# Gated DeltaNet and squared-ReLU MLP layer in float32 on one core: where the substitution rows, the query norms and the output roots of a head pair stand in the program

## Chip, cores and metric

One core of a Trainium2 chip runs the whole kernel. The metric is the device time of one execution in microseconds (us). Most executions agree within 0.3%.

## What is computed

The input x is one sequence of 2048 tokens with 1024 features, in float32. DEPTH is 1, so there is one layer: RMS norm, gated DeltaNet mixer, residual, RMS norm, squared-ReLU MLP (1024 to 4096 to 1024), residual, and a final RMS norm. The reference of the mixer, cut to what matters:

```python
def gated_deltanet(h, w_in, conv_w, a_log, dt_bias, norm_w, w_out):
    proj = h @ w_in
    qkv = silu(causal_depthwise_conv(proj[..., :3 * DN_WIDTH], conv_w))      # 4 taps
    z, b, a = rest_of(proj)
    q, k, v = split(qkv)                                                     # 8 heads of 128
    q, k = l2_normalize(q), l2_normalize(k)
    beta, g = sigmoid(b), -exp(a_log) * softplus(a + dt_bias)
    o = chunk_gated_delta_rule(q, k, v, beta, g)
    o = o * rsqrt(mean(o * o) + eps) * norm_w * silu(z)
    return o @ w_out

def chunk_gated_delta_rule(q, k, v, beta, g):          # per head and chunk
    lower = strict_lower(k_beta @ k.T * decay)
    u, w = solve(I + lower, [v * beta, k_beta * exp(gc)])
    attn = (q @ k.T) * decay
    # then, chunk after chunk:
    v_new = u - w @ state
    o_c = q_dec @ state + attn @ v_new
    state = state * g_last + k_dec.T @ v_new
```

## The kernel before, in words

The kernel works on chunks of 128 tokens. The sequence goes in two blocks of 1024 tokens (`TB`). For each block `mixer` runs, then `mlp_block`. A mixer has two halves of 512 tokens (`s` = 0, 1), and each half has four pairs of heads (`HP` = 2), so there are 16 pairs in all, of 8 chunk matrices each (`NC` = 2 heads times 4 chunks).

**One pair.** Six projections (`conv_part`, counted by n = 1 to 6: k, q and v of both heads) are each 24 matmuls of 128x512 on PE (`dense`, L117 to L119: each float32 product is three matmuls of split parts). ACT then copies the PSUM bank twice (L302, L303), DVE runs three taps of the convolution (L306), ACT a tanh (L309) and DVE the last product (L310). After n = 3 and n = 4 `key_matrices` makes the strictly lower matrices `mt`. Also after n = 4, `invert_diagonal` (L312) starts to invert the 32x32 diagonal blocks: ACT spreads `mt` into `xc` by four copies (L320), DVE transposes it (L323), and 31 substitution rows follow, each one product and one reduction on DVE (L330, L332). After n = 5 and n = 6 `query_norms` (L436) squares the queries of one head on ACT (`sq`, L440) and sums them on PE by four thin matmuls with a column of ones (L442). DVE adds epsilon (L444).

**The pair before it.** When all six projections of a pair are recorded, `wind_up` (L582) handles the previous pair: `prepare2` calls `invert`, which completes the 128x128 inverse from the small blocks by 32-wide and 64-wide matmuls (L358, L365, L368, L377, L382) with copies `z` on ACT between (L360, L379). It also transposes k and v (L457) and makes the attention matrix (L465). `chain` is the recurrence over four chunks (L483 to L500), and after it come the root mean squares of the output (L505 to L513), one head after the other, each with its own `rsqrt` (L126). `gate` projects the gate z of both heads, 24 matmuls of 128x512 each; these wide matmuls stand between the small ones of `invert` and `chain`. `finish` transposes the output and multiplies it by the gate.

**What sets the order.** A scheduler takes the instructions in the order in which the code records them, as a priority, and lays out one fixed queue for each engine, so that an instruction recorded late can stand earlier on an engine that would otherwise idle by the scheduler's own estimates. On the chip each engine works through its queue in order, and whatever stands behind a waiting instruction waits too. PSUM banks: two for projections (`pj`), two for most small products (`kq`), two for the recurrence (`ch`), two for outputs (`po`).

Of the kernel before, what the change touches and what calls it, by code (L numbers as in the profile page):

```python
# [7 lines left out]
F32 = mybir.dt.float32  # L8
# [25 lines left out]
def tile_kernel(ctx: ExitStack, tc: tile.TileContext, x, w_in, w_out, w_up, w_down, n_mlp, n_fin, consts, out):  # L34
# [274 lines left out]
        act.activation(th, dst, AF.Tanh, scale=0.5)  # L309
        dve.scalar_tensor_tensor(dst, th, 1.0, dst, op0=ADD, op1=MULT)  # L310

    def invert_diagonal(ap, mt):  # L312

        R = 32 // NC
        xc = wp.tile([P, 32, R, NC], F32, name="xc", tag="xt", bufs=4)
        for b in range(4):
            r = slice(32 * b, 32 * b + 32)
            act.copy(xc[r], mt[r, :, 32 * b:32 * b + 32].rearrange("p t i -> p i t").unsqueeze(2)  # L320
                     .to_broadcast([32, 32, R, NC]))
        pr = wp.tile([P, 32, 32], F32, name="pr", tag="xt", bufs=4)
        dve.transpose(pr.rearrange("p i j -> p (i j)"), xc.rearrange("p i r t -> p (i r t)"))  # L323
        pool.memset(pr.rearrange("p i j -> p (i j)")[:, 0:1024:33], 1.0)
        tt = ap.tile([P, NC, 32], F32, name="tt", tag="tt")
        pool.tensor_copy(tt.rearrange("p c j -> p (c j)"), e0)
        tmp = ap.tile([P, NC, 32], F32, name="tmp", tag="tmp", bufs=1)
        for i in range(1, 32):
            n = i // R + 1
            dve.tensor_tensor(tmp[:, 0:n, 0:i + 1], tt[:, 0:n, 0:i + 1],  # L330
                              pr[:, i, 0:i + 1].unsqueeze(1).to_broadcast([P, n, i + 1]), op=MULT)
            dve.tensor_reduce(tt[:, 0:n, i], tmp[:, 0:n, 0:i + 1], axis=mybir.AxisListType.X, op=ADD)  # L332
        return tt

    def invert(ap, mt, tt, uf, t64):

# [49 lines left out]
    def sl(t):  # L386
        return slice(t * P, (t + 1) * P)
# [55 lines left out]
        c = NC + j * HT  # L443
        dve.tensor_scalar_add(u["n2"][:, c:c + HT], ps[:, 0:HT], 4.0 * EPS)  # L444

    def prepare2(ap, sb, h, q2, k2, v2, gt, u, ub, t64):
        c0 = h * HT
        dt_, rk = u["dt"], u["rk"]
        invert(ap, u["mt"], u["tt"], ub, t64)
        qe = row(ap, eg_d, "qe", sb, c0)  # L450
        (dve if c0 == NH * HT - NC and sb % 2 else pool).tensor_tensor(flat(qe), flat(qe), q2, op=MULT)
        kt, vt = head(ap, "kt"), head(ap, "vt")
        for dst, src, sc in ((vt, v2, lambda c: rk[:, c:c + 1]), (kt, k2, lambda c: gt["egl"][:, c0 + c:c0 + c + 1])):
            for hf in range(2):
                ps = big("kq")
                for t in range(HT):
                    pe.transpose(ps[:, sl(t)], src[:, sl(hf * HT + t)], ident)  # L457
                for t in range(HT):
                    c = hf * HT + t
                    act.activation(dst[:, c, :], ps[:, sl(t)], AF.Copy, scale=sc(c))  # L460
        for hf in range(2):
            ps = big("kq")
            for t in range(HT):
                s = sl(hf * HT + t)
                pe.matmul(ps[:, sl(t)], k2[:, s], q2[:, s], start=True, stop=True)  # L465
            cs = slice(hf * HT, (hf + 1) * HT)
            dve.tensor_tensor(flat(dt_[:, cs, :]), ps, flat(dt_[:, cs, :]), op=MULT)
        u.update(ub=ub, qe=qe, kt=kt, vt=vt, at=dt_, k2=k2, gt=gt, c0=c0)

    def chain(ap, h0, u):  # L470

        def col(name, c):
            return u["gt"][name][:, u["c0"] + c:u["c0"] + c + 1]
# [2 lines left out]
        for t in range(HT):  # L476
            ts_ = slice(t * P, (t + 1) * P)
            cs = [j * HT + t for j in range(HP)]
            st = [S[h0 + j] for j in range(HP)]
            ys, vrs = [], []  # L480
            for j, c in enumerate(cs):
                ps = big("ch")
                pe.matmul(ps[:, 0:P], u["k2"][:, c * P:(c + 1) * P], st[j], start=True, stop=True)  # L483
                y = ap.tile([P, P], F32, name="y", tag="y")
                dve.scalar_tensor_tensor(y, ps[:, 0:P], col("neg", c), u["vt"][:, c, :], op0=MULT, op1=ADD)
                ys.append(y)
            for j, c in enumerate(cs):
                pe.matmul(po[j][:, ts_], u["qe"][:, c, :], st[j], start=True, stop=False)
            for j, c in enumerate(cs):
                ps = big("ch")  # L490
                pe.matmul(ps[:, 0:P], u["ub"][:, c, :], ys[j], start=True, stop=True)
                vr = ap.tile([P, P], F32, name="vr", tag="vr")
                act.activation(vr, ps[:, 0:P], AF.Copy, scale=u["cc"][:, c:c + 1])
                vrs.append(vr)
            for j, c in enumerate(cs):
                ps = big("ch")
                pe.matmul(ps[:, 0:P], u["kt"][:, c, :], vrs[j], start=True, stop=True)
                dve.scalar_tensor_tensor(st[j], st[j], col("egt", c), ps[:, 0:P], op0=MULT, op1=ADD)
            for j, c in enumerate(cs):
                pe.matmul(po[j][:, ts_], u["at"][:, c, :], vrs[j], start=False, stop=True)  # L500
        os_ = []
        for j in range(HP):
            ms = sm.tile([P, HT], F32, name="ms", tag="ms")
            o = ap.tile([P, HT, P], F32, name="o", tag="o")
            for t in range(HT):  # L505
                act.activation(o[:, t, :], po[j][:, t * P:(t + 1) * P], AF.Square, accum_out=ms[:, t:t + 1])
            nq = sm.tile([P, HT], F32, name="nq", tag="nq")
            dve.tensor_scalar_mul(nq, u["n2"][:, NC + j * HT:NC + (j + 1) * HT], EPS * P)
            dve.scalar_tensor_tensor(nq, ms, 1.0 / P, nq, op0=MULT, op1=ADD)
            rq = sm.tile([P, HT], F32, name="rq", tag="rq")  # L510
            rsqrt(rq, nq)
            for t in range(HT):
                act.activation(o[:, t, :], po[j][:, t * P:(t + 1) * P], AF.Copy, scale=rq[:, t:t + 1])  # L513
            os_.append(o)
        return os_

    def gate(ap, hT, h, sb):
# [51 lines left out]
    def mixer(blk, hT):  # L569
        with tc.tile_pool(name="ap", bufs=2) as ap:  # L570
# [8 lines left out]
                    finish(*r)  # L579
                ready.clear()  # L580

            def wind_up(sb, h, hT, qkv, gt, u):  # L582
                prepare2(ap, sb, h, *qkv, gt, u, ub, t64)
                os_ = chain(ap, h, u)
                return [(sb, h + j, os_[j], gate(ap, hT, h + j, sb)) for j in range(HP)]

            gt = None
            for s in range(2):
                sb = 2 * blk + s
                for h in range(0, NH, HP):  # L590
# [3 lines left out]
                    for part in (1, 0, 2):  # L594
                        d = ap.tile([P, HP * HB], F32, name=f"c{part}", tag=f"c{part}")
                        qkv.append(d)
                        for j in range(HP):
# [12 lines left out]
                            if n == 4:  # L610
                                key_matrices(u, qkv[0], 1)
                                key_norms(u)
                                u["tt"] = invert_diagonal(ap, u["mt"])
                                finish_ready()
                            if n == 5:
                                query_norms(ap, u, qkv[1], 0)
                            if n == 6:
                                query_norms(ap, u, qkv[1], 1)
                            if blk == 0 and s == 1 and n in (2, 5):
                                split_out(h // HP * 2 + n // 5)  # L620
                            if s == 0 and n == 1:
# [241 lines left out]
```

## Time and profile before

| | us |
|---|---|
| three runs, median | 3015.39 |
| three runs, lowest and highest | 3009.5 and 3017.04 |
| the profiled execution, its own time | 3014.35 |
| its span in the profile | 3012.3 |
| PE busy | 2845.6 (94%) |
| DVE busy | 1582.8 (53%) |
| ACT busy | 1023.5 (34%) |
| POOL busy | 731.6 (24%) |

The span is the time from the first to the last instruction; 2.05 us of the execution lie around it. Times in the trace count from the start of the span. PE is the matmul engine; a busy PE can still run at half its clock, so its busy share has to be read together with the granted clock (PEclk). The two mixers stand at about 40 to 760 us and 1590 to 2205 us, the MLP stages after each of them.

### The profile page before, as it was taken

The page shows a single profiled execution, that of the slowest core. Times are in us where ns is not written, and L with a number is a line of the kernel's source. Part 1 is how long each engine was busy: PE and PEld are TensorE (multiplying, and loading weights), DVE is VectorE, ACT ScalarE, POOL GpSimd, SP SyncE. Part 2 cuts the span into 40 slices and gives each one's busy share as a digit, 9 for nine tenths or more (in the row PEclk, how much of TensorE's full clock was granted, in tenths as well). Part 3 has the DMA queues.
Part 4 walks back from the last instruction along what each step waited for, and adds up shares of the span by engine and source line. Part 5 has one row for each costly group of instructions (what it writes and reads, how often), then busy time and mean ns, then how long its engine had stood idle before and what let it go on. Part 6 is the DMA issues. An engine that isn't in the chain of part 4 may idle for free.

```text
span 3012.3 us, 40577 instructions
## 1 busy us (share of the span) xinstructions
PE 2845.6 (94%) x15352; PEld 2390.5 (79%) x15352; DVE 1582.8 (53%) x4054; ACT 1023.5 (34%) x2338; POOL 731.6 (24%) x646
## 2 busy tenths in 40 slices
PE   7888989889999999999999999999999999999998
PEld 5677777778978888888887778888888888888887
DVE  7787676665333333333387767666543333333334
ACT  4454544444221111111146555554532111111112
POOL 6443221110043323323311111010003233233221
PEclk9888988889999999999999999888899999999999
DMA  6544443446621111111144334333563111111111
GB/s 254 171 152 153 144 161 140 161 172 210 215 75 49 36 56 55 43 43 56 57 167 177 127 119 148 132 122 129 173 214 126 43 57 46 39 56 52 46 43 63
DMA packets 81844, 337.66 MB, mean 112 GB/s; under 512 B 8816, under 2 KB 17264, under 8 KB 60144
## 3 DMA queue, kind: packets, MB, share of 16 engines
q1 hardware_dynamic: 60528, 292.98, 28.6%
q10 hardware_dynamic: 21120, 42.08, 4.1%
q8 instruction: 121, 1.98, 0.3%
q14 instruction: 75, 0.61, 0.1%
HBM read 271.98 MB, written 63.05 MB: 111 GB/s over the span
## 4 chain that ended last, share of the span: by engine, by line
PE 75%; DVE 11%; ACT 8%; DMA 3%; issue 2%; POOL 1%; ACTq 0%; DVEq 0%; SPq 0%; POOLq 0%
PE pj L117 14%; PE pj L119 14%; PE pj L118 13%; PE kq L119 4%; PE ch L119 4%; PE kq L118 4%; PE kq L117 4%; PE ch L118 4%; PE ch L117 4%; ACT xc L320 3%; DVE c L306 2%; DMA w<-wo 1%; DMA orw<-o_d 1%; PE kq L457 1%; PE kq L442 1%
## 5 line engine op out<-in xcount | busy, mean ns | idle before, releaser
L117 PE MATMUL pj<-hh,w 128*128 128x512 f32 x2048 | 841.1, 411 | 23.1 <-DVE z2s L521 10.3
L119 PE MATMUL pj<-hl,w 128*128 128x512 f32 x2048 | 836.5, 409 | 0.0
L118 PE MATMUL pj<-hh,w 128*128 128x512 f32 x2048 | 833.8, 407 | 0.0
L117 PEld LDWEIGHTS pj<-hh,w 128*128 128x128 f32 x2048 | 401.8, 196 | 106.4 <-DVE z2s L521 12.8
L118 PEld LDWEIGHTS pj<-hh,w 128*128 128x128 f32 x2048 | 401.3, 196 | 79.6 <-issue 0.4
L119 PEld LDWEIGHTS pj<-hl,w 128*128 128x128 f32 x2048 | 399.8, 195 | 80.9
L709 ACT ACTIVATE r<-pj 128x512 f32<-128x512 f32 x128 | 76.8, 600 | 1068.5 <-PE pj L119 1068.5
L712 DVE TENSOR_TENSOR ul<-r,uh 128x512 fp32r<-128x512 f32 x128 | 130.4, 1019 | 491.4 <-ACT uh L711 491.4
L306 DVE SCALAR_TENSOR_TENSOR c<-raw,cst,c 128x512 f32<-128x512 f32 x288 | 251.4, 873 | 62.7 <-ACT c L303 46.6
L90 POOL TENSOR_SCALAR w<-wr 128x1024 fp32r<-128x1024 f32 x106 | 115.4, 1089 | 648.5 <-PE pj L119 424.6
L91 POOL TENSOR_TENSOR w<-wr,w 128x1024 fp32r<-128x1024 f32 x106 | 260.8, 2460 | 6.6
L90 POOL TENSOR_SCALAR dh<-wr 128x1024 fp32r<-128x1024 f32 x62 | 64.4, 1057 | 653.4 <-PE ch L118 611.0
L119 PE MATMUL ch<-dl,uh 128*128 128x512 f32 x496 | 193.7, 390 | 1.4 <-POOL dl L91 1.4
L117 PE MATMUL ch<-dh,uh 128*128 128x512 f32 x496 | 193.7, 391 | 0.0
L118 PE MATMUL ch<-dh,ul 128*128 128x512 f32 x496 | 193.7, 391 | 0.0
L119 PE MATMUL kq<-dl,uh 128*128 128x512 f32 x496 | 193.6, 390 | 0.0
L118 PE MATMUL kq<-dh,ul 128*128 128x512 f32 x496 | 193.4, 390 | 0.0
L117 PE MATMUL kq<-dh,uh 128*128 128x512 f32 x496 | 193.2, 390 | 0.0
L752 DVE TENSOR_TENSOR x<-kq,x 128x512 f32<-128x512 f32 x128 | 88.4, 691 | 159.6 <-PE kq L119 159.5
L117 PE MATMUL pj<-w,hh 128*128 128x256 f32 x512 | 149.9, 293 | 11.5 <-DMA w<-wo 7.0
L91 POOL TENSOR_TENSOR dl<-wr,dh 128x1024 fp32r<-128x1024 f32 x62 | 147.5, 2403 | 0.3
L119 PE MATMUL pj<-w,hh 128*128 128x256 f32 x512 | 147.5, 288 | 0.0
(319 smaller groups left out, 4654.1 us busy)
## 6 DMA issues: line engine op xcount, KB each, us to landing
w<-wi SPq DMA_DIRECT2D x96, 1024.0 KB, 5.0
wi<-w SPq DMA_DIRECT2D x32, 1024.0 KB, 4.8
wr<-in_w_up SPq DMA_DIRECT2D x64, 512.0 KB, 3.6
w<-wo SPq DMA_DIRECT2D x32, 1024.0 KB, 6.6
wr<-in_w_down SPq DMA_DIRECT2D x64, 512.0 KB, 3.5
wr<-in_w_in SPq DMA_DIRECT2D x32, 512.0 KB, 5.8
qe<-eg_d ACTq DMA_DIRECT2D x16, 512.0 KB, 3.8
o_d<-z2s ACTq DMA_DIRECT2D x32, 256.0 KB, 3.1
```

What stands on the lines that cost most here:

```text
L90: pool.tensor_scalar(dst_h, src, 1.0, 0.0, op0=MULT, op1=ADD)
L91: pool.tensor_tensor(dst_l, src, dst_h.bitcast(F32), op=SUB)
L117: pe.matmul(ps, ah, bh, start=first and i == 0, stop=False)
L118: pe.matmul(ps, al, bh, start=False, stop=False)
L119: pe.matmul(ps, ah, bl, start=False, stop=last and i == n - 1)
L306: dve.scalar_tensor_tensor(dst, raw[:, k:k + HB], cw[:, 4 * f + k:4 * f + k + 1], dst, op0=MULT, op1=ADD)
L320: act.copy(xc[r], mt[r, :, 32 * b:32 * b + 32].rearrange("p t i -> p i t").unsqueeze(2) .to_broadcast([32, 32, R, NC]))
L442: pe.matmul(ps[:, t:t + 1], sq[:, sl(t)], ones[:, 0:1], start=True, stop=True)
L457: pe.transpose(ps[:, sl(t)], src[:, sl(hf * HT + t)], ident)
L709: act.activation(r, ps, AF.Relu)
L712: dve.tensor_tensor(ul[:, hs], r, uh[:, hs].bitcast(F32), op=SUB)
L752: dve.tensor_tensor(dst, ps, dst, op=ADD)
```

## The change

The diff, its core:

```diff
-    def invert_diagonal(ap, mt):
+    def invert_diagonal(ap, u):
...
         pool.tensor_copy(tt.rearrange("p c j -> p (c j)"), e0)
+        yield
         tmp = ap.tile([P, NC, 32], F32, name="tmp", tag="tmp", bufs=1)
         for i in range(1, 32):
...
             dve.tensor_reduce(tt[:, 0:n, i], tmp[:, 0:n, 0:i + 1], axis=mybir.AxisListType.X, op=ADD)
-        return tt
+            if i % 2 or i > 16:
+                yield
+        u["tt"] = tt
...
-    def prepare2(ap, sb, h, q2, k2, v2, gt, u, ub, t64):
+    def prepare2(ap, sb, h, q2, k2, v2, gt, u, ub, t64, fill):
...
                     act.activation(dst[:, c, :], ps[:, sl(t)], AF.Copy, scale=sc(c))
+                fill(1)
...
             dve.tensor_tensor(flat(dt_[:, cs, :]), ps, flat(dt_[:, cs, :]), op=MULT)
+            fill(1)
...
-    def chain(ap, h0, u):
+    def chain(ap, h0, u, fill):
...
                 ys.append(y)
+            fill(3)
...
                 dve.scalar_tensor_tensor(st[j], st[j], col("egt", c), ps[:, 0:P], op0=MULT, op1=ADD)
+            fill(2)
...
-        os_ = []
+        os_ = [ap.tile([P, HT, P], F32, name="o", tag="o") for _ in range(HP)]
+        ms = sm.tile([P, NC], F32, name="ms", tag="ms")
...
-            nq = sm.tile([P, HT], F32, name="nq", tag="nq")
-            dve.tensor_scalar_mul(nq, u["n2"][:, NC + j * HT:NC + (j + 1) * HT], EPS * P)
-            dve.scalar_tensor_tensor(nq, ms, 1.0 / P, nq, op0=MULT, op1=ADD)
-            rq = sm.tile([P, HT], F32, name="rq", tag="rq")
-            rsqrt(rq, nq)
+        nq = sm.tile([P, NC], F32, name="nq", tag="nq")
+        dve.tensor_scalar_mul(nq, u["n2"][:, NC:2 * NC], EPS * P)
+        dve.scalar_tensor_tensor(nq, ms, 1.0 / P, nq, op0=MULT, op1=ADD)
+        rq = sm.tile([P, NC], F32, name="rq", tag="rq")
+        rsqrt(rq, nq)
...
-            def wind_up(sb, h, hT, qkv, gt, u):
-                prepare2(ap, sb, h, *qkv, gt, u, ub, t64)
-                os_ = chain(ap, h, u)
+            def wind_up(sb, h, hT, qkv, gt, u, rows_of=iter(())):
+
+                def fill(n):
+                    for _ in range(n):
+                        next(rows_of, None)
+
+                fill(1)
+                prepare2(ap, sb, h, *qkv, gt, u, ub, t64, fill)
+                for j in range(HP):
+                    query_norms(ap, u, qkv[0], j)
+                os_ = chain(ap, h, u, fill)
...
-                                u["tt"] = invert_diagonal(ap, u["mt"])
+                                rows_of = invert_diagonal(ap, u)
                                 finish_ready()
-                            if n == 5:
-                                query_norms(ap, u, qkv[1], 0)
-                            if n == 6:
-                                query_norms(ap, u, qkv[1], 1)
...
                     if prev is not None:
-                        ready += wind_up(*prev)
+                        ready += wind_up(*prev, rows_of)
+                    for _ in rows_of:
+                        pass
```

`invert_diagonal` becomes a generator; `wind_up` of the previous pair draws the current pair's spreading, transposition and substitution rows from it, a few at a time, between its own steps: one portion at its start, one after each of four transpose groups and two attention products, three after the two y of a chunk and two after its two state updates. The query norms of a pair are recorded in its own `wind_up`, just ahead of its `chain`. The roots of both heads' outputs are taken in one pass of eight columns. Line numbers of the changed kernel are 4 higher from `invert` on and 6 to 9 higher from the middle of `chain` on.

What the scheduler makes of it is shown at three places, all of one pair in the second half of the second block. First PE's queue, from the last wide matmul of projection n = 6 (weights w_16667 before) to the second group of 32-wide matmuls of `invert` (L358; `sq` holds the squared queries, `tcm` the small inverses, S the states). Before:

```order
L119 MATMUL pj<-hl,w_16667 128x512
L483 MATMUL ch<-S_84,c_15588 128x128
L483 MATMUL ch<-S_86,c_15588 128x128
L488 MATMUL po<-S_84,qe 128x128
L442 MATMUL kq<-ones,sq 128x1 x4
L358 MATMUL kq<-tcm,mt 32x32 x8
L488 MATMUL po<-S_86,qe 128x128
L117 MATMUL pj<-hh,w_17009 128x512
L118 MATMUL pj<-hh,w_17009 128x512
L119 MATMUL pj<-hl,w_17009 128x512
L117 MATMUL pj<-hh,w_17009 128x512
L358 MATMUL kq<-tcm,mt 32x32 x8
```

The same stretch of PE's queue in the changed kernel (n = 6 has the weights w_16330, L358 is now L362, L483 and L488 are L489 and L495):

```order
L119 MATMUL pj<-hl,w_16330 128x512
L362 MATMUL kq<-tcm,mt 32x32 x8
L489 MATMUL ch<-S_84,c_15352 128x128
L489 MATMUL ch<-S_86,c_15352 128x128
L495 MATMUL po<-S_84,qe 128x128
L495 MATMUL po<-S_86,qe 128x128
L117 MATMUL pj<-hh,w_16733 128x512
L118 MATMUL pj<-hh,w_16733 128x512
L119 MATMUL pj<-hl,w_16733 128x512
L362 MATMUL kq<-tcm,mt 32x32 x8
```

The query norm has left this stretch, the first 32-wide group comes straight after the projection, and three wide matmuls of the gate instead of four lie ahead of the second group.

Second, ACT's queue of the same pair, from the evacuation of projection n = 5 (`raw` and the v part c_16619) to the first copies `z` of `invert`. Before:

```order
L302 COPY raw<-pj 128x512
L303 ACTIVATE c_16619<-pj,cst 128x512
L320 COPY xc<-mt 32x1024 x4
L309 ACTIVATE raw<-c_16619 128x512
L440 ACTIVATE sq<-c_16403 128x512
L302 COPY raw<-pj 128x512
L303 ACTIVATE c_16619<-pj,cst 128x512
L360 COPY z<-kq 32x256 x2
```

And in the changed kernel:

```order
L302 COPY raw<-pj 128x512
L303 ACTIVATE c_16290<-pj,cst 128x512
L321 COPY xc<-mt 32x1024 x3
L309 ACTIVATE raw<-c_16290 128x512
L321 COPY xc<-mt 32x1024
L302 COPY raw<-pj 128x512
L303 ACTIVATE c_16290<-pj,cst 128x512
L364 COPY z<-kq 32x256 x2
```

The square is gone from between the spreading copies and `z`; the four spreading copies and the evacuation of n = 6 still stand ahead of `z`.

Third, PE's queue of the same pair at the first chunk of the recurrence in the changed kernel (L470 is the attention product, L504 and L508 take `vr`, the new values of the chunk):

```order
L470 MATMUL kq<-c_15427,c_15352 128x128 x4
L446 MATMUL kq<-ones,sq 128x1 x4
L504 MATMUL ch<-vr,kt 128x128 x2
L508 MATMUL po<-vr,dt__15465 128x128
L118 MATMUL pj<-hh,w_16733 128x512
L446 MATMUL kq<-ones,sq 128x1 x4
L508 MATMUL po<-vr,dt__15465 128x128
L119 MATMUL pj<-hl,w_16733 128x512
L489 MATMUL ch<-S_84,c_15352 128x128
```

Both thin groups of the query norms (L446) now stand here.

## Rows read from the trace of the kernel before

**Rows 1.** The page: PE's line of busy times, and the strip of its granted clock over the span in 40 slices (9 is full speed, 8 and 7 are means with stretches at half).

```profile
PE 2845.6 (94%) x15352; PEld 2390.5 (79%) x15352; DVE 1582.8 (53%) x4054; ACT 1023.5 (34%) x2338; POOL 731.6 (24%) x646
PEclk9888988889999999999999999888899999999999
```

**Rows 2.** Busy time by stretch, the first and the second mixer: stretch, its length, busy us and instructions of each engine, granted clock, DMA share, GB/s.

```profile
40.00:760.00 720.00, 631.00 (x3840) 530.01 (x3839) 507.47 (x1506) 343.89 (x840) 187.44 (x198) 0.88 0.48 167
1590.00:2205.00 615.00, 579.25 (x3706) 490.61 (x3705) 416.48 (x1434) 333.18 (x813) 58.84 (x123) 0.91 0.41 142
```

**Rows 3.** Who PE waited for over the whole span: us in total, times, longest.

```profile
PE kq L442 <- ACT sq L440: 48.3, 12, 5.0
PE kq L419 <- DVE hl L190: 25.2, 6, 7.7
...
PE pj L117 <- DVE z2s L521: 10.3, 6, 3.4
...
PE kq L442 <- DVE mt L429: 3.5, 3, 1.7
```

**Rows 4.** Timeline of PE through the same pair whose queues are shown above: start, duration, line, operation, and in brackets the idle time before it and what ended it.

```profile
1947.36 0.40 PE L119 MATMUL pj<-hl,w 128*128 128x512 f32 x1
1947.60 0.95 PE L442 MATMUL kq<-ones,sq 128*128 128x1 f32 x8
1948.40 0.48 PE L117 MATMUL pj<-hh,w 128*128 128x512 f32 x1
...
1953.75 0.40 PE L119 MATMUL pj<-hl,w 128*128 128x512 f32 x1
...
1958.20 1.86 PE L442 MATMUL kq<-ones,sq 128*128 128x1 f32 x8 [3.39 <-ACT sq L440]
1960.00 1.05 PE L358 MATMUL kq<-tcm,mt 32*32 32x32 f32 x16
...
1963.41 0.79 PE L358 MATMUL kq<-tcm,mt 32*32 32x32 f32 x11
...
1974.38 0.66 PE L457 MATMUL kq<-cst,c 128*128 128x128 f32 x4
```

**Rows 5.** Timeline of ACT through the same stretch.

```profile
1947.85 0.59 ACT L302 COPY raw<-pj 128x512 f32<-128x512 f32 x1 [2.66 <-PE pj L119]
...
1948.91 8.06 ACT L320 COPY xc<-mt 32x1024 f32<-32x1024 f32 x4
1957.00 0.63 ACT L309 ACTIVATE raw<-c 128x512 f32<-128x512 f32 x1
1957.54 0.61 ACT L440 ACTIVATE sq<-c 128x512 f32<-128x512 f32 x1
1958.06 0.57 ACT L302 COPY raw<-pj 128x512 f32<-128x512 f32 x1
1958.52 0.69 ACT L303 ACTIVATE c<-pj,cst 128x512 f32<-128x512 f32 x1
1961.09 0.36 ACT L360 COPY z<-kq 32x256 f32<-32x256 f32 x1 [1.88 <-PE kq L358]
```

**Rows 6.** Busy time by stretch, columns as in rows 2: five stretches of `invert` and `chain`. The column after the five engines is the granted clock.

```profile
1806.70:1818.00 11.30, 11.30 (x149) 9.14 (x147) 6.26 (x35) 4.21 (x9) 0.43 (x2) 1.00 0.27 94
1960.00:1974.00 14.00, 14.00 (x125) 10.96 (x124) 6.17 (x26) 3.03 (x7) 0.19 (x1) 0.50 0.00 1
1654.00:1662.00 8.00, 8.00 (x121) 6.27 (x119) 4.77 (x25) 5.46 (x14) 0.23 (x2) 1.00 0.09 37
142.00:154.00 12.00, 12.00 (x98) 8.91 (x97) 3.95 (x22) 4.58 (x12) 0.40 (x1) 0.50 0.42 145
...
1980.00:1995.00 15.00, 15.00 (x103) 13.69 (x102) 13.99 (x43) 5.10 (x24) 2.11 (x1) 1.00 0.37 126
```

**Rows 7.** Timeline of PE in two other pairs: the first 32-wide group of one, the second group and the first transposes of the other.

```profile
1653.79 0.69 PE L358 MATMUL kq<-tcm,mt 32*32 32x32 f32 x16 [2.59 <-ACT tcm L341]
...
1810.43 0.59 PE L358 MATMUL kq<-tcm,mt 32*32 32x32 f32 x13
...
1817.97 0.66 PE L457 MATMUL kq<-cst,c 128*128 128x128 f32 x4
```

**Rows 8.** Timeline of DVE in a recurrence: a step y of the chain (L485), a substitution row's product and reduction, a state update (L498).

```profile
1905.40 0.35 DVE L485 SCALAR_TENSOR_TENSOR y<-ch,neg,vt 128x128 f32<-128x128 f32 x1
1905.67 0.29 DVE L330 TENSOR_TENSOR tmp<-tt,pr 128x138 f32<-128x138 f32 x1
...
1906.47 0.29 DVE L332 TENSOR_REDUCE tt<-tmp 128x6 f32<-128x138 f32 x1
1906.82 0.35 DVE L498 SCALAR_TENSOR_TENSOR S<-S,egt,ch 128x128 f32<-128x128 f32 x1
```

**Rows 9.** Timelines of DVE and of POOL at the output roots of a pair in the first block.

```profile
608.11 2.37 DVE L509 SCALAR_TENSOR_TENSOR nq<-ms,nq 128x4 f32<-128x4 f32 x1 [0.29 <-ACT o L506]
...
611.83 2.13 DVE L137 TENSOR_TENSOR rt<-rq 128x4 f32<-128x4 f32 x1
...
615.41 0.16 DVE L137 TENSOR_TENSOR rt<-rq 128x4 f32<-128x4 f32 x1
...
608.05 2.40 POOL L451 TENSOR_TENSOR qe<-qe,c 128x1024 f32<-128x1024 f32 x1 [25.98 <-DMA qe<-eg_d]
...
611.55 2.40 POOL L91 TENSOR_TENSOR w<-wr,w 128x1024 fp32r<-128x1024 f32 x1
```

More of the change, by code (lines that the diff above doesn't have):

```diff
@@ L310, in conv_part @@
         dve.scalar_tensor_tensor(dst, th, 1.0, dst, op0=ADD, op1=MULT)
-    def invert_diagonal(ap, mt):
+    def invert_diagonal(ap, u):
         R = 32 // NC
+        mt = u["mt"]
         xc = wp.tile([P, 32, R, NC], F32, name="xc", tag="xt", bufs=4)
@@ L498, in chain @@
                 dve.scalar_tensor_tensor(st[j], st[j], col("egt", c), ps[:, 0:P], op0=MULT, op1=ADD)
+            fill(2)
             for j, c in enumerate(cs):
                 pe.matmul(po[j][:, ts_], u["at"][:, c, :], vrs[j], start=False, stop=True)
-        os_ = []
+        os_ = [ap.tile([P, HT, P], F32, name="o", tag="o") for _ in range(HP)]
+        ms = sm.tile([P, NC], F32, name="ms", tag="ms")
         for j in range(HP):
-            ms = sm.tile([P, HT], F32, name="ms", tag="ms")
-            o = ap.tile([P, HT, P], F32, name="o", tag="o")
             for t in range(HT):
-                act.activation(o[:, t, :], po[j][:, t * P:(t + 1) * P], AF.Square, accum_out=ms[:, t:t + 1])
-            nq = sm.tile([P, HT], F32, name="nq", tag="nq")
-            dve.tensor_scalar_mul(nq, u["n2"][:, NC + j * HT:NC + (j + 1) * HT], EPS * P)
-            dve.scalar_tensor_tensor(nq, ms, 1.0 / P, nq, op0=MULT, op1=ADD)
-            rq = sm.tile([P, HT], F32, name="rq", tag="rq")
-            rsqrt(rq, nq)
+                c = j * HT + t
+                act.activation(os_[j][:, t, :], po[j][:, t * P:(t + 1) * P], AF.Square, accum_out=ms[:, c:c + 1])
+        nq = sm.tile([P, NC], F32, name="nq", tag="nq")
[4 more added lines that the diff above has]
+        for j in range(HP):
             for t in range(HT):
-                act.activation(o[:, t, :], po[j][:, t * P:(t + 1) * P], AF.Copy, scale=rq[:, t:t + 1])
-            os_.append(o)
+                c = j * HT + t
+                act.activation(os_[j][:, t, :], po[j][:, t * P:(t + 1) * P], AF.Copy, scale=rq[:, c:c + 1])
         return os_
@@ L580, in finish_ready @@
                 ready.clear()
-            def wind_up(sb, h, hT, qkv, gt, u):
-                prepare2(ap, sb, h, *qkv, gt, u, ub, t64)
-                os_ = chain(ap, h, u)
+            def wind_up(sb, h, hT, qkv, gt, u, rows_of=iter(())):
[4 more added lines that the diff above has]
+                prepare2(ap, sb, h, *qkv, gt, u, ub, t64, fill)
+                for j in range(HP):
+                    query_norms(ap, u, qkv[0], j)
+                os_ = chain(ap, h, u, fill)
                 return [(sb, h + j, os_[j], gate(ap, hT, h + j, sb)) for j in range(HP)]
```

## The prediction

> **What bounds the kernel now.** I read the page first: PE is busy for 94% of the span [rows 1]. Its clock strip is the more telling line: it reads 9 and 8 in the two mixer stretches and full speed nearly everywhere else [rows 1]. So the mixers are where time can come from. By stretch, the first mixer has 89 us in which PE idles (720 less 631.00) and the second 36 us (615 less 579.25), at mean clocks of 0.88 and 0.91 [rows 2]. Since the clock has two levels, 1.2 and 2.4 GHz, a mean of 0.88 over 720 us is 2 x 0.12 x 720 = 173 us at the lower one, and 0.91 over 615 us is 111 us.
>
> Next, the list of PE's waits. The longest is for the query norm: L442 waits for `sq` 12 times, 48.3 us in all [rows 3], which is in 12 of 16 pairs. The timeline shows one of them: after the last wide matmul of n = 6 and the first products of the recurrence, PE stands for 3.39 us until L442 can start [rows 4]. ACT's timeline says why: `sq` is not long (0.61 us), but it stands behind four spreading copies of 8.06 us together [rows 5]. Then the clock: the stretch behind this wait runs at 0.50, at the lower level, while a pair that enters the same stretch at 2.4 GHz keeps 1.00 [rows 6]. From the second 32-wide group to the first transposes the slow pair takes 1974.38 - 1963.41 = 10.97 us [rows 4], the fast one 1817.97 - 1810.43 = 7.54 us with some gate products of its own in it [rows 7].
>
> DVE and ACT are not full: in the second mixer DVE is busy 416.48 of 615 us and ACT 333.18 [rows 2].
>
> **The substitution rows: nothing.** The change's words are about interleaving them with the recurrence. But the scheduler does that already: between a y and a state update of the chain DVE runs a row's product and its reduction [rows 8]. Recording them there states an order that the queue already has, so I cost it at nothing; what hides them are the chain's own waits. Were that cover gone, a row's product and reduction would put 0.58 us (2 x 0.29) [rows 8] into a step of the chain. The spreading copies keep their place on ACT behind the evacuation of n = 5, as its queue shows.
>
> **The query norms: the wait moves.** With L442 gone from behind n = 6, PE goes on with the first 32-wide group, four products, three wide matmuls, and then needs the second 32-wide group. That group writes the bank from which ACT takes the first `z`, and `z` stands behind the same four spreading copies. So what is late next is `z`.
>
> When does it end? The copies start at 1948.91 as before, since what precedes them on ACT is unchanged. Add 8.06 for the copies, about 0.55 for L309 and 1.15 for the two evacuations of n = 6 (starts of 1957.00, 1957.54, 1958.06 and ends at 1959.2), and 0.36 for `z` [rows 5]: 1959.05, and the second group at about 1959.2 instead of 1963.41 [rows 4], 4.2 us earlier. PE gets there early: n = 6 starts at 1947.60 instead of 1948.40, so ends 0.8 us earlier than before, at 1953.2. The first group (1.05 us at half the clock [rows 4], so about 0.5) and four products (about 0.23 each, as a wide matmul) take some 1.5 us at full clock, three wide matmuls 0.7 (0.24 us apart in [rows 4], 1947.36 to 1947.60), so PE stands from 1955.4 to 1959.2: **3.8 us, as long as before**, on another line.
>
> From the 4.2 us goes what now comes later: two thin groups at 0.80 us each (1947.60 to 1948.40) [rows 4] and a wide matmul at 0.23, 1.8 us together. They stand in the first chunk of the recurrence, where PE is busy without a gap (15.00 of 15.00 us) [rows 6], so they count in full. DVE's epsilon additions (L444, now L448) come between the state updates of that chunk; the thin group is done about as early as the products they would otherwise wait for, so I add nothing, with an upper end of 1 us. Net 2.4 us a pair, **29 us** for 12. Ends: nothing, if the thin groups and the chain behind them cost 4.2; the whole 4.2, or 50 us, if they fill gaps.
>
> **The clock.** I take it that a wait of 3.8 us lowers the clock as the wait of 3.39 us did, and that the small matmuls behind it stay at 1.2 GHz to about the same place: the gain above counts that. A wait of 2.59 us at the first 32-wide group [rows 7] left the clock at 1.00 in the stretch behind it [rows 6], so the bound on the other side is no fall at all; 3.8 is nearer to 3.39, and beyond it.
>
> **The first pair of each block.** There L442 waits for `mt`, 3.5 us in three times [rows 3]; nothing else stands behind that wait in the changed queue. I add **5 us**, ends 3 and 10, the upper end if the slow clock behind it goes as well.
>
> **The output roots.** One pass instead of two leaves out 13 small DVE instructions a pair. Their means mislead: in [rows 9] one takes 2.37 us and another 2.13, a like one 0.16, and the long ones end with POOL's two-input products (608.05 + 2.40 and 611.55 + 2.40). POOL's work does not change, so such a pause passes to whichever instruction stands there. What goes is 13 x 0.16 = 2.1 us of DVE, of which about half stands ahead of the gate's product z2s, for which PE waits 10.3 us in six times, the longest 3.4 [rows 3]. I take **3 us**, three long waits by 1 us; ends 0 and 10. Against it: the first head's output now waits for the second's squares; `finish` needs both only in the next pair, which hides it.
> The Trainium skill ("SBUF — State Buffer", Who interferes with whom) says that a VectorE instruction with two SBUF inputs contends with a GpSimd instruction that reads SBUF, and that the later one is blocked until the other ends. By that rule the pauses stay, as I took it; counted as work they would give 2.37 + 2.13 us a pair more. The trace agrees with the rule: 608.11 + 2.37 = 610.48 against 610.45.
>
> **Sum.** 29 + 5 + 3 = 37 us off the profiled 3014.35 us is 2977; that execution is 1 us below the median of the runs, so **2978 us** against 3015.39, 1.2% less. Its own range: 2958 (50 + 10 + 10 would be 2944, but not all ends together) to 3003. About 0.3% (9 us) is what a measurement of this kernel can tell from no change.
>
> **Rivals.**
> *The clock stays up* (2937 us). The wait at `z` could come out under 3 us, as one of 2.59 us did no harm [rows 6, 7]. For it: six wide matmuls instead of three precede the second group in some pairs, 0.7 us less waiting. Against it: 3.8 us. Price: 10.97 - 7.54 = 3.4 us, with the gate products of about 1 us in the fast pair 4.4; in about 9 pairs, 40 us more than the forecast.
>
> *The clock does not come back before the recurrence* (3058 us, slower). Before, it is at 1.00 in the recurrence after a slow `invert` [rows 6]. Now the slow stretch contains less work at its start and two thin groups follow in the first chunk. If 1.2 GHz lasts through the recurrence, its 15 us at 1.00 [rows 6], about 9 us of it bound by PE's columns, cost 9 us more a pair: 81 in 9 pairs, less 37, is 44 us slower. It decides from about 4 us a pair upward. Against it: the wide matmuls between the transposes raised the clock before, and they stand ahead of the thin groups still.
> The Trainium skill ("TensorE: Matmul & The Clock Gate", What's actually happening) has it that the throttled state is the default and activity releases it. By that rule a sparser stretch delays the release, and the time would be this rival's. The trace agrees as far as it goes: 0.50 lasts through the small matmuls and ends among the wide ones; how sparse is too sparse no row shows.
>
> *The wait only changes its name* (3015 us). If the thin groups, their epsilon additions and a longer `z` wait eat the 4.2 us. For it: PE's queue is one line and everything taken out comes back in. Against it: L442 and the first group ran at 1.2 GHz behind the wait, 1.86 and 1.05 us [rows 4], and the thin ones now run at 2.4.
>
> **Chances.** Forecast 52%, clock up 20%, wait renamed 15%, clock late 13%. Faster by over 0.3%: the first two and a little of the third's lower edge, 0.73; within it 0.14; slower 0.13. The range from 2925 to 3017 takes in the forecast, the renamed wait and most of the clock-up case, and leaves out the slow one and the far end of the fast one.
>
> **What would show it.** Right: no PE wait on the query norm, a new one of about 12 x 3.8 = 45 us in which the second 32-wide group waits for `z`; the thin groups without a wait in the first chunk; 0.50 still in the `invert` of most pairs; no new DVE wait in the recurrence. Wrong: `z` early because the spreading copies moved; a clock of 1.00 through `invert`, or of 0.50 in the recurrence; PE waiting for a state update behind an epsilon addition.

## The result, and the profile after

| | median us (lowest to highest) | ratio to before, 95% interval |
|---|---|---|
| before | 3015.39 (3009.5 to 3017.04) | |
| changed | 2986.29 (2982.07 to 2998.89) | 0.9914 (0.9888 to 0.9940) |

The change takes 0.9% off; the forecast was 1.2%. The profiled execution of the changed kernel spans 2986.9 us, 25.4 us less than before.

The page after, PE's line and the strip of its clock:

```profile
PE 2816.9 (94%) x15352; PEld 2367.1 (79%) x15352; DVE 1567.0 (52%) x3846; ACT 1029.9 (34%) x2338; POOL 733.0 (25%) x646
PEclk9888888999999999999999999999999999999999
```

Against [rows 1], PE issues the same 15352 matmuls and is busy 28.7 us less. Span less busy time is 3012.3 - 2845.6 = 166.7 us before and 2986.9 - 2816.9 = 170.0 us now. **PE stands still no less than before; its work has become faster.** The clock record of the trace accounts for it: of PE's busy time 273.3 us stood at the lower level before and 217.1 us now, and half of the difference is 28.1 us.

The two mixers by stretch, columns as in [rows 2]:

```profile
40.00:760.00 720.00, 626.64 (x3959) 528.17 (x3957) 508.08 (x1406) 349.87 (x850) 187.84 (x198) 0.90 0.49 172
1590.00:2205.00 615.00, 576.42 (x3819) 493.13 (x3818) 408.13 (x1326) 328.38 (x814) 52.51 (x116) 0.93 0.42 145
```

The clock rose from 0.88 to 0.90 and from 0.91 to 0.93 [rows 2]. Who PE waited for:

```profile
PE kq L362 <- ACT z L364: 43.0, 12, 5.8
PE kq L423 <- DVE hl L190: 17.8, 5, 5.8
PE kq L362 <- ACT tcm L345: 15.7, 2, 11.5
PE kq L186 <- DVE xn L181: 13.5, 2, 9.3
...
PE pj L117 <- DVE z2s L530: 10.8, 5, 3.2
```

No wait for `sq` is left of the 48.3 us in [rows 3]. In its place the second 32-wide group waits for `z`, 12 times, 43.0 us. Two waits in the first pairs are new or longer (`xn` and `tcm`).

A pair at the place of [rows 4], PE's timeline:

```profile
1937.87 0.69 PE L362 MATMUL kq<-tcm,mt 32*32 32x32 f32 x16
...
1939.94 0.40 PE L119 MATMUL pj<-hl,w 128*128 128x512 f32 x1
1944.12 0.90 PE L362 MATMUL kq<-tcm,mt 32*32 32x32 f32 x13 [3.77 <-ACT z L364]
...
1954.17 0.66 PE L461 MATMUL kq<-cst,c 128*128 128x128 f32 x4
...
1960.25 0.95 PE L446 MATMUL kq<-ones,sq 128*128 128x1 f32 x8
...
1962.05 0.95 PE L446 MATMUL kq<-ones,sq 128*128 128x1 f32 x8
```

ACT through the same stretch, to be held against [rows 5]:

```profile
1933.07 0.70 ACT L303 ACTIVATE c<-pj,cst 128x512 f32<-128x512 f32 x1
1933.65 6.08 ACT L321 COPY xc<-mt 32x1024 f32<-32x1024 f32 x3
1939.76 0.63 ACT L309 ACTIVATE raw<-c 128x512 f32<-128x512 f32 x1
1940.41 1.94 ACT L321 COPY xc<-mt 32x1024 f32<-32x1024 f32 x1
1942.38 0.59 ACT L302 COPY raw<-pj 128x512 f32<-128x512 f32 x1
1942.99 0.69 ACT L303 ACTIVATE c<-pj,cst 128x512 f32<-128x512 f32 x1
1943.70 0.36 ACT L364 COPY z<-kq 32x256 f32<-32x256 f32 x1
```

The first 32-wide group is done at 1938.6, but its evacuation `z` stands behind four spreading copies and starts at 1943.70. PE waits 3.77 us for it. The thin groups of the query norm now run without a wait in the recurrence. The clock around this wait, columns as in [rows 2]:

```profile
1944.00:1953.00 9.00, 8.88 (x89) 6.95 (x89) 5.56 (x23) 2.73 (x7) 0.20 (x1) 0.50 0.01 2
1953.00:1966.00 13.00, 13.00 (x106) 11.91 (x106) 8.62 (x35) 7.34 (x23) 0.00 (x0) 1.00 0.01 2
```

The clock still falls at the wait, and is back at 1953. In the four pairs wound up in this half the low stretch lasted 6.8 to 13.7 us, against 17.1 to 20.5 before. DVE in a recurrence does the same as in [rows 8], rows between y (L491) and state update (L505):

```profile
1890.03 0.35 DVE L491 SCALAR_TENSOR_TENSOR y<-ch,neg,vt 128x128 f32<-128x128 f32 x1
1890.30 0.28 DVE L332 TENSOR_TENSOR tmp<-tt,pr 128x126 f32<-128x126 f32 x1
...
1890.61 0.29 DVE L334 TENSOR_REDUCE tt<-tmp 128x6 f32<-128x126 f32 x1
...
1891.47 0.34 DVE L505 SCALAR_TENSOR_TENSOR S<-S,egt,ch 128x128 f32<-128x128 f32 x1
```

Where the 25.4 us came from, by the times at which each pair's output products (L500, now L508) begin. The end of a mixer is taken here behind its output projection and the transposes that follow (L211), and the last stretch ends with the last matmul, 9.0 us ahead of the span's end in both:

| stretch | before | changed |
|---|---|---|
| start to the first pair's products | 163.1 | 162.9 |
| block 1, pair 1 to pair 4 (s = 0) | 261.2 | 262.0 |
| block 1, pair 4 to pair 7 (s = 1) | 256.1 | 246.3 |
| block 1, pair 7 to the end of the mixer | 185.0 | 176.8 |
| MLP and block 2 to its first pair's products | 803.6 | 804.8 |
| block 2, pair 1 to pair 4 | 234.3 | 234.5 |
| block 2, pair 4 to pair 7 | 234.4 | 224.9 |
| block 2, pair 7 to the end of the mixer | 179.3 | 179.3 |
| the rest | 686.3 | 686.4 |

The gain stands in the second halves, 3.2 us for each of six pairs, and in the end of the first mixer. The first halves gained nothing: there 98.3 us of PE's busy time stood at the lower level before and 97.9 us now. In the second halves it was 108.9 and is 68.3, half of which difference is 20.3 us.

### The profile page after: what moved, and what is told of

It is laid out like the page before. It is cut to its first block, busy times and chain, and to the rows that moved or that the text cites. A ratio compares the mean times of both kernels' runs of the same rounds, so it can differ in the third digit from the quotient of the medians.

```text
span 2986.9 us, 40297 instructions
## 1 busy us (share of the span) xinstructions
PE 2816.9 (94%) x15352; PEld 2367.1 (79%) x15352; DVE 1567.0 (52%) x3846; ACT 1029.9 (34%) x2338; POOL 733.0 (25%) x646
## 5 line engine op out<-in xcount | busy, mean ns | idle before, releaser
L117 PE MATMUL pj<-hh,w 128*128 128x512 f32 x2048 | 834.5, 407 | 21.6 <-DVE z2s L530 10.8
L119 PE MATMUL pj<-hl,w 128*128 128x512 f32 x2048 | 826.9, 404 | 0.0
L117 PEld LDWEIGHTS pj<-hh,w 128*128 128x128 f32 x2048 | 397.6, 194 | 107.9 <-DVE z2s L530 9.6
L118 PEld LDWEIGHTS pj<-hh,w 128*128 128x128 f32 x2048 | 397.1, 194 | 78.1 <-issue 0.4
L727 DVE TENSOR_TENSOR ul<-r,uh 128x512 fp32r<-128x512 f32 x128 | 120.6, 942 | 494.1 <-ACT uh L726 494.1
L119 PE MATMUL kq<-dl,uh 128*128 128x512 f32 x496 | 193.6, 390 | 0.0
L332 DVE TENSOR_TENSOR tmp<-tt,pr 128x2 f32<-128x2 f32 (+30 forms) x496 | 157.0, 317 | 9.5 <-POOL pr L325 0.5
L117 PE MATMUL pj<-w,hh 128*128 128x256 f32 x512 | 148.7, 290 | 8.9 <-DMA w<-wo 8.2
```

What stands on the lines that cost most here:

```text
L117: pe.matmul(ps, ah, bh, start=first and i == 0, stop=False)
L118: pe.matmul(ps, al, bh, start=False, stop=False)
L119: pe.matmul(ps, ah, bl, start=False, stop=last and i == n - 1)
L727: dve.tensor_tensor(ul[:, hs], r, uh[:, hs].bitcast(F32), op=SUB)
```

## The experiments

Each ran on one chip beside the kernel before, whose medians there were 3011.58 (first four), 3011.88, 3012.01 and 3013.54 us. "Still" is the profiled span less PE's busy time; the last column is PE's wait for `sq` and for the first `z`. The last three columns are of one execution each; that of e5, e8 and e10 took 2994.45, 2999.79 and 3001.43 us, 9 to 12 us more than the median.

| run | median | ratio, 95% interval | PE busy | still | sq, z |
|---|---|---|---|---|---|
| before | 3015.39 | | 2845.6 | 166.7 | 48.3, - |
| changed | 2986.29 | 0.9914 (0.9888 to 0.9940) | 2816.9 | 170.0 | -, 43.0 |
| e1 norms only | 3002.43 | 0.9975 (0.9964 to 0.9986) | 2827.6 | 171.8 | -, 45.8 |
| e2 generator only | 2985.72 | 0.9917 (0.9903 to 0.9930) | 2805.5 | 174.7 | 8.0, 33.6 |
| e3 roots only | 3014.81 | 1.0015 (0.9999 to 1.0030) | 2840.6 | 166.1 | 52.3, - |
| e4 spreading on POOL | 2987.07 | 0.9924 (0.9906 to 0.9941) | 2809.7 | 171.9 | -, 35.1 |
| e5 late, at once | 2982.45 | 0.9907 (0.9888 to 0.9926) | 2818.4 | 174.2 | 8.7, 34.4 |
| e6 early, rows drawn | 3016.93 | 1.0021 (1.0010 to 1.0033) | 2843.2 | 170.4 | 51.2, - |
| e7 spreading at the gate | 2972.34 | 0.9870 (0.9852 to 0.9888) | 2788.9 | 182.9 | 0.3, 3.7 |
| e8 first rows at once | 2990.43 | 0.9925 (0.9910 to 0.9940) | 2834.0 | 164.0 | -, 43.2 |
| e9 changed, at the gate | 2954.38 | 0.9817 (0.9797 to 0.9837) | 2788.4 | 167.7 | -, 0.6 |
| e10 at the gate, halves | 2989.49 | 0.9932 (0.9915 to 0.9949) | 2810.7 | 188.9 | 0.2, 3.4 |
| e11 spreading doubled | 3026.56 | 1.0059 (1.0041 to 1.0077) | 2828.1 | 193.6 | -, 69.5 |
| e12 at the gate, and roots | 2962.88 | 0.9832 (0.9807 to 0.9857) | 2784.6 | 175.1 | -, 2.5 |

**e1: the query norms moved, nothing else.** In the kernel before:

```diff
-                            if n == 5:
-                                query_norms(ap, u, qkv[1], 0)
-                            if n == 6:
-                                query_norms(ap, u, qkv[1], 1)
...
                 prepare2(ap, sb, h, *qkv, gt, u, ub, t64)
+                for j in range(HP):
+                    query_norms(ap, u, qkv[0], j)
```

> The kernel before with one part of the change alone: the query norms recorded in wind_up, ahead of the chain. Theory (the norms are the whole of it, and their wait moves to the copies z): 2985 to 2995 us, ratio 0.990 to 0.994 to the kernel before; no PE wait of L442 on sq, and some 40 us in 12 waits of the second 32-wide group (L358) on z. Rival (the interleaving carries the gain): 3010 to 3020 us, no change. Second rival (the parts need each other, the norms alone make the recurrence later): 3020 us or more.

PE's new wait in e1, in all, times and longest:

```profile
PE kq L358 <- ACT z L360: 45.8, 14, 5.2
```

The wait moves to `z` as forecast, but only 0.25% comes of it, 7.5 us of 3011.58. Between the second-half pairs the gain is there (from pair 4 to pair 7 of block 1, 245.1 us against 256.1). From pair 7 to the ends of the mixers e1 takes 187.3 and 184.2 us, 15.4 more than the changed kernel (176.8 and 179.3) and 7.2 more than the kernel before (185.0 and 179.3). So 8.2 of the 15.4 us are a gain of the changed kernel that the norms alone do not make; what costs e1 the other 7.2 stays open.

**e2: the generator only**, drawn by `wind_up`; norms and roots as before.

> The kernel before with the substitution rows drawn in portions by wind_up, and nothing else of the change. Theory (the scheduler had the rows between the steps of the recurrence already): within 9 us of 3015, the wait of the query norm on sq still near 48 us in 12. Rival (the interleaving carries the gain): 2985 to 2995 us with that wait still there. Second rival (it costs: the spreading copies and rows of the pairs in a block's first half come later): 3025 us or more.

It has the whole gain of the change, and the forecast had put this part at nothing. So either the drawing of the rows gains, or the place of the spreading copies, which stand in the generator's first portion.

**e3: the roots in one pass, nothing else.**

> The kernel before with the output roots of both heads in one pass, and nothing else of the change. Theory (POOL's pauses stay and pass to other instructions): 3008 to 3015 us, PE's wait on the gate product z2s about 7 instead of 10.3 us. Rival (the long small instructions go with the second pass, about 4 us a pair in the first block): 2985 us.

No gain: 1.0015.

**e4: the changed kernel with the spreading on POOL.**

```diff
-            act.copy(xc[r], mt[r, ...
+            pool.tensor_copy(xc[r], mt[r, ...
```

> The changed kernel with the four spreading copies xc of each pair (L321) on POOL instead of ACT. Theory (z is late because it stands behind these copies on ACT, and the clock falls because of that wait): the wait of the second 32-wide group on z, 43.0 us before, under 10 us; granted clock 1.00 in invert in most pairs; 2890 to 2915 us, some 45 us for the wait and 30 to 50 for the clock. Rival A (the wait passes to another instruction once more): the z wait gone, another of about the same size in its place, 2975 to 2990 us. Rival B (the clock falls in invert because its matmuls are small, not because of the wait): the wait gone, 0.50 in invert still, 2935 to 2950 us. Rival C (the copies are slow on POOL, and the convolution's tails behind them hold ACT): over 2990 us.

The time is the changed kernel's. POOL's timeline and DVE's, in the same pair:

```profile
1928.35 9.16 POOL L321 COPY xc<-mt 32x1024 f32<-32x1024 f32 x4
```
```profile
1928.85 6.88 DVE L306 SCALAR_TENSOR_TENSOR c<-raw,cst,c 128x512 f32<-128x512 f32 x3 [0.88 <-ACT c L303]
```

DVE's timeline in the changed kernel:

```profile
1933.87 2.33 DVE L306 SCALAR_TENSOR_TENSOR c<-raw,cst,c 128x512 f32<-128x512 f32 x3 [0.88 <-ACT c L303]
```

With POOL at the copies, three taps of the convolution take 6.88 us; in the changed kernel three take 2.33 us. The tanh behind them on ACT is late, and `z` behind that: PE waits 2.65 us in this pair. The Trainium skill ("SBUF — State Buffer", Who interferes with whom) says that a VectorE instruction with two SBUF inputs contends with a GpSimd instruction that reads SBUF; the trace agrees, 2.29 us a tap and 2.29 us a copy. So POOL was no place for the copies.

**e5 and e6 take e2 apart.** e5 records spreading and rows in one piece at the start of `wind_up`; e6 draws the first portion, the spreading, at n = 4 and only the rows in `wind_up`:

```diff
e5
-                fill(1)
+                fill(99)
e6
                                 rows_of = invert_diagonal(ap, u)
+                                next(rows_of)
...
-                fill(1)
```

> Before, with the spreading and all substitution rows recorded in one piece at the start of wind_up (not at n = 4), so nothing is drawn between the steps of the recurrence; norms and roots as before. Theory A (only the place of the spreading copies counts: they now stand on ACT behind both squares, so the wait of the query norm goes, as in the rows-only kernel): about 0.992 of before, PE wait on sq under 10 us, busy time at the low clock near 185 us. Theory B (the drawing of the rows between the steps of the recurrence gains): no better than before, ratio 1.00 or above, DVE rows in front of state updates.

> Before, with the spreading at n = 4 as before and only the rows drawn between the steps of the recurrence; norms and roots as before. Theory A (place of the spreading copies): ratio 1.00 (0.997 to 1.003), the wait of the query norm on sq still about 48 us in 12 times, busy time at the low clock near 270 us. Theory B (drawing of the rows): about 0.992.

ACT's timeline in e5 and then in e6 (`sq` is L444 in both):

```profile
1934.34 0.69 ACT L303 ACTIVATE c<-pj,cst 128x512 f32<-128x512 f32 x1
1934.92 0.63 ACT L444 ACTIVATE sq<-c 128x512 f32<-128x512 f32 x1
1935.44 4.12 ACT L321 COPY xc<-mt 32x1024 f32<-32x1024 f32 x2
```
```profile
1949.42 8.06 ACT L321 COPY xc<-mt 32x1024 f32<-32x1024 f32 x4
1957.51 0.63 ACT L309 ACTIVATE raw<-c 128x512 f32<-128x512 f32 x1
1958.05 0.61 ACT L444 ACTIVATE sq<-c 128x512 f32<-128x512 f32 x1
```

Theory A holds for the time as a whole: the rows drawn between the steps give nothing (1.0021), the later record of the spreading gives all (0.9907). Recorded after n = 6, the copies have a lower priority than the squares, so `sq` goes ahead of them and the wait on it falls from 48.3 to 8.7 us.

**e7: spreading and rows recorded behind the recurrence**, on the base of e2, so that they stand neither ahead of `sq` nor of `z`; the spreading comes ahead of the gate products, the rows after them:

```diff
-                fill(1)
-                prepare2(ap, sb, h, *qkv, gt, u, ub, t64, fill)
-                os_ = chain(ap, h, u, fill)
+                prepare2(ap, sb, h, *qkv, gt, u, ub, t64, lambda n: None)
+                os_ = chain(ap, h, u, lambda n: None)
+                fill(1)
```

> Before, with the spreading and the rows recorded behind the recurrence, ahead of the gate products, so that ACT has no spreading copy ahead of the squares or of z. Theory C (the low clock comes from the one long wait at the spreading copies): no PE wait on sq, none of over 1 us on z in the last three pairs of a block, busy time at the low clock from 185 us in the rows-only kernel to under 100, PE idle 30 us less: about 2920 us, ratio 0.97. Rival D (the low clock belongs to the thin matmuls of the inversion, whatever the wait): the wait goes but low-clock time stays near 185, about 2955 us, ratio 0.98. Rival E (8 us of copies now stand ahead of the evacuations of kt, vt and vr): new waits there of 2 to 4 us a pair, time as before or above, ratio 0.99 to 1.01.

Three stretches of the second half, of the kernel before, the changed one and e7, which hold much the same pairs:

```profile
1840.00:2080.00 240.00, 229.21 (x1387) 194.09 (x1387) 161.03 (x540) 121.58 (x297) 25.74 (x52) 0.88 0.37 131
```
```profile
1840.00:2080.00 240.00, 228.69 (x1442) 194.71 (x1441) 166.94 (x513) 126.13 (x296) 24.07 (x56) 0.92 0.39 137
```
```profile
1840.00:2080.00 240.00, 227.78 (x1588) 191.29 (x1586) 164.35 (x542) 138.25 (x324) 28.27 (x53) 0.99 0.42 143
```

With the wait gone the clock stays at 0.99 through the same thin matmuls: here D is refuted, and C's cause is shown. In 240 us PE starts 1588 matmuls in place of 1387. Over the whole execution C's figures were not reached: 130.7 us of PE's busy time still stood at the lower level (C said under 100), and the median is 2972 for 2920. Rival E, new waits behind the copies, came too, each smaller than its price:

```profile
PE ch L498 <- DVE y L491: 20.9, 14, 1.5
...
PE kq L461 <- ACT ub L388: 14.6, 11, 1.5
```

The copies now stand ahead of `ub` and among the evacuations of the recurrence, up to 1.5 us at each place, 35.5 us in all. And from pair 7 to the ends of the mixers e7 takes 198.1 and 197.2 us, 31 more than before, with 53.2 us at the lower level there against 20.4. Both bear on what parts 2972 from 2920; why the ends of the mixers lose, no run shows.

**e8: the changed kernel with the first pair's rows recorded at once at n = 4.**

> The changed kernel, but the rows of the first pair of a block, which has no neighbour to be drawn by, recorded at once at n = 4 as before. Theory F (in the first pair the rows come too late or pile up on DVE ahead of the normalized tokens, whence the new waits of 9.3 and 11.5 us in block 0 and 4.1 and 4.2 us in block 1): both waits back to about 2.8 and 2.6 us, 10 to 20 us off the changed kernel, about 2970 us, ratio 0.987. Rival G (they come from the first pair's other work): 2986 us, waits unchanged.

The wait for `xn` falls from 9.3 to 2.6 us and the one for `tcm` from 11.5 to 7.8, so F names the right cause of the first. But the first pair's products begin only 3.6 us sooner (159.3), and the time is no better. In this execution waits of 3.8 us on `z` were followed by low stretches of 13.7 to 17.1 us in four pairs of the second block (10.2 to 13.7 in three of the changed kernel). It took 9 us more than the median, so whether such stretches make up for the gain in the others is not shown, nor why they are longer.

**e9: the changed kernel with e7's edit.**

> The changed kernel (norms in wind_up, one pass of roots) with the spreading and the rows recorded behind the recurrence, ahead of the gate products. Theory C (the wait at the spreading copies and the low clock behind it are what the changed kernel still pays): no wait of z over 1 us in the last pairs of a block, low clock in TensorE's busy time from 217 us to about 135 as in the kernel of before so treated, about 2970 us, ratio 0.986. Rival H (the squares now come on ACT between the last spreading copies and the evacuations vr, in the recurrence): a wait for vr or for the query norm of 2 to 4 us a pair in its place, 2985 us or more.

2954 us, 1.8% less than before: the lowest median of all, and faster than the changed kernel, with no overlap of the intervals. Hardly a wait for `z` is left, 0.6 us, and rival H did not come: PE waits 0.4 us for `vr`, and for the norm less than 0.15 us at a time. The mixers, at 0.93 and 0.98:

```profile
40.00:760.00 720.00, 634.77 (x4111) 535.23 (x4110) 516.24 (x1447) 353.36 (x864) 189.32 (x198) 0.93 0.50 177
1590.00:2205.00 615.00, 575.67 (x4010) 492.40 (x4009) 406.64 (x1313) 325.19 (x814) 56.15 (x109) 0.98 0.44 154
```

The ends of the mixers are what is left: from pair 7 on e9 takes 197.5 and 196.0 us, 37 more than the changed kernel.

**e10: e7 with each spreading copy cut in two** (16 of 32 rows each).

> Before with the spreading behind the recurrence, and each of its four copies cut in two halves of 1 us. Theory: the two waits of 1.1 to 1.5 us a pair that stood in the uncut form behind two whole copies (kt and vt evacuations, and y) become under 1 us each: 16 pairs by about 1.5 us, 20 us less than the uncut form, about 2950 us, ratio 0.980. Rival: the queue takes five halves in one place instead of two wholes, so the wait there grows by 1 us and the other shrinks by 0.5: 2972 us, 0.987.

Worse than e7, and worse than either theory said. ACT's copies in the recurrence of one pair in e7, and the same place in e10 (line numbers are 2 higher there):

```profile
2003.40 4.01 ACT L321 COPY xc<-mt 32x1024 f32<-32x1024 f32 x2
```
```profile
2020.66 0.74 ACT L502 ACTIVATE vr<-ch,cc 128x128 f32<-128x128 f32 x2
2021.42 5.22 ACT L322 COPY xc<-mt 32x512 f32<-32x512 f32 x5
2026.67 0.62 ACT L502 ACTIVATE vr<-ch,cc 128x128 f32<-128x128 f32 x2
```

PE's waits at the copies in e10:

```profile
PE ch L506 <- ACT vr L502: 26.1, 14, 2.3
...
PE kq L463 <- ACT ub L390: 8.4, 11, 1.0
```

The scheduler put five halves (5.22 us) where two wholes (4.01 us) had stood. One wait grew and the other shrank, as the rival said, but in sum they are as in e7, 34.5 us against 35.5, and do not explain the loss. Of the 27.8 us between the two spans 20.2 lie from pair 7 to the ends of the mixers (208.1 and 207.4 us), with 78.7 us at the lower level there for e7's 53.2. Why, no run shows.

**e11: two of the four copies made twice**, in the changed kernel.

> The changed kernel with two of the four spreading copies made twice, 4 us more on ACT a pair at the same place. If what stands ahead of z sets the wait, it grows from 3.8 to about 7.8 us in the last pairs of a block; 12 to 14 pairs by 4 us is 48 to 56 us, about 3040 us if the stretch at the low clock behind it stays as long (ratio 1.009), 3060 if it grows too. Rival: z is late for another reason, 2986 us (0.992).

PE's wait for `z` in e11 (line numbers are 3 higher):

```profile
PE kq L365 <- ACT z L367: 69.5, 15, 6.9
```

The wait for `z` grows from 43.0 to 69.5 us, and the time by 1.5% against the changed kernel. So what stands ahead of `z` on ACT sets the wait. In a last pair `z` starts 3.9 us later behind the first 32-wide group, but the wait grows by 2.1 us only (5.87 for 3.77): PE has eleven wide matmuls ahead of the second group in place of three, eight more by 0.23 us. Both terms move, 24 us more standing still and 11 us more busy.

**e12: e7 with the roots in one pass**, the norms where they were.

> Before with the spreading and the rows behind the recurrence, and both heads' roots in one pass, but the query norms where they were (behind n = 5 and n = 6). It tells which of the other two parts of the change is worth the 18 us by which the changed kernel with late spreading beats the kernel of before with late spreading. If the one pass of roots (fewer small DVE instructions ahead of z2s where the rows now stand among them): about 2955 us, ratio 0.982, the waits for z2s under 10 us. If the place of the query norms: about 2972 us, 0.987, z2s waits as without the one pass (14 us in four long ones in block 0). Each half: 2963.

0.9832 lies between e7 and e9 and nearer to e9, but its interval overlaps with both. Which part is worth how much there stays open.

## Why the prediction was right, and where not

**What bounds the kernel**: right. The gain is all clock, in the mixers, and the `sq` wait was the place; e7 shows for the second half of block 2 that without a long wait at the spreading copies the clock does not fall.

**The substitution rows, nothing**: right for the rows as a whole (e6, 1.0021), and this part failed in its last sentence. It followed the spreading copies' place in the changed kernel's queue, where they stand behind the same evacuation as before, and took that as all that their new record could do. e2 and e5 show that the later record alone lifts `sq` over the copies and has the whole gain. In the changed kernel it has no `sq` left to lift, since the norms are gone from there. In the second halves the two edits repair the same wait and do not add up: from pair 4 to pair 7 of both blocks e1 takes off 19.5 us, e2 18.5 and both together 19.3. For the whole time that is not shown: 0.9975 x 0.9917 is 0.9892, inside the changed kernel's interval.

**The query norms, 29 us**: the mechanism was right: 3.8 us on `z` forecast and 3.77 measured in the pair that it was worked out for (1.96 to 5.79 over the twelve); 45 us in 12 waits forecast, 43.0 in 12 measured; thin groups without a wait. The size was not. A second-half pair gains 3.2 us for the forecast's 2.4, by the shorter stretch at the low clock, but a first-half pair gains none, so that six pairs give 19.3 us instead of twelve 29. In the first halves the clock was low for as long as before; why it was not there as in the second, no run shows. Alone, the norms gave 7.5 us (e1). A count of waits is not a count of pairs that gain.

**The first pair, 5 us**: failed, 0.2 us in block 1. I had said that nothing else stood behind that wait. The rows of the first pair, which has no neighbour to draw them, are recorded behind n = 6, and PE now waits for `xn` (9.35 us) and `tcm` (11.51 us); e8 takes most of the first away and a third of the second. In e1, without the generator, the first pair's products begin at 157.9, 5.2 us sooner; but in e3, which changes nothing there, at 160.6, so one execution cannot show a term of this size.

**The output roots, 3 us**: not measurable (e3, 1.0015; `z2s` waits 10.8 us for 10.3 [rows 3]).

**The sum**: 37 forecast, 25.4 in the spans. Terms: 19.3 for 29, none for 5 and 3; 8.2 us at the end of the first mixer were in no term. That the total came as near as it did is in part luck: without these it would be 17.2. They go with the drawing of the rows: from pair 7 to the end of the first mixer the kernels that draw them take 176.7 to 180.9 us (changed, e2, e4, e6, e8, e11), those that record them in one piece ahead of the recurrence 185.0 to 189.0 (before, e1, e3, e5). In e6 it is lost again elsewhere, 4.3 us in the first half before it and 4.4 in the MLP behind it.

**The rivals.** "The clock stays up" put its point at 3 us because a wait of 2.59 us did no harm [rows 6, 7]. In e5, waits of 2.4 us in the last pairs of block 2 were followed by 6.8 to 13.7 us at the low level: one row is no threshold. "The clock does not come back": 1.00 from 1953, inside `invert`; no. Its counter-argument misread the trace: in the kernel before, the clock was back at 1973.9, ahead of the first transposes (1974.38 [rows 4]), so the wide matmuls between these had not raised it. "The wait only changes its name" is true of the waiting, 170.0 us for 166.7, and wrong of the time: behind the same wait the low stretch of the second halves is shorter, with the query norm's thin groups gone from it.

## What to carry to other kernels

Compare PE's busy time at an equal number of matmuls before counting waits: here every version stood still for 164 to 194 us, and most of the gains were clock. Where a long block of an in-order queue stands ahead of short copies that the matmul engine needs, moving what waits only renames the wait; move the block, to where little waits behind it (e9), not to an engine whose copies hold up another that the short copies wait for (e4). Under a scheduler the place of a record is a priority: test the record of each piece apart from the idea that it serves (e5, e6).

## What the runs showed of the hardware

A wait of this kind cost more than its length: e7 has 56.7 us less PE busy time than before with the long waits at the spreading copies gone, though PE stood still 16 us longer in all. The cost varied: after waits of 3.8 us the low level lasted 10.2 to 17.1 us (changed and e8), after 2.4 us 6.8 to 13.7 (e5). POOL copies of 2.29 us stretched DVE instructions of 0.78 us (2.33 for three) to the same 2.29 (e4).
